# A two-layer trunk in split fp32: three conditioning vectors summed by transfers, residuals on VectorE, and tails of products in another order

## The chip, the cores and the metric

The kernel runs on one core of one Trainium2 chip. The metric is the device time of one execution in microseconds (us), the median of the runs shown. TensorE (PE) multiplies matrices; VectorE (DVE), ScalarE (ACT) and GpSimd (POOL) work on tiles; SyncE (SP) issues most of the transfers (DMA). Each engine carries out its own instructions in program order and waits for the others at semaphores.

## The reference

256 tokens of 1024 elements pass two layers. Each layer has a mixer and a "peer" block, each between a modulation and a residual with a layer norm. All is float32, batch 1.

```python
for i in range(2):
    sh1, sc1, g1, sh2, sc2, g2 = split(silu(c) @ ada_w[i] + ada_b[i], 6)   # conditioning vectors of 1024
    hx = xs * (1 + sc1) + sh1
    if i == 0:                       # mixer 0: hc is the modulated context
        q, k, v, gu, gv = split(hx @ w_in); k_c, v_c = split(hc @ w_in[:, 1024:3072])
        a = head_rms(softmax(q1 k1) v - lam * softmax(q2 k2) v)       # 8 heads, rope on q and k
        yx = concat(a, gelu(gu) * spatial(layer_norm(gelu(gv)))) @ w_out
    else:                            # mixer 1: window means as a fixed 256x256 matrix per group
        yx = (grouped(multiscale_pool(hx @ w_in), w_grp) * scale) @ w_out
    xs = layer_norm(alpha * xs + g1 * yx) * ln_g[i,0] + ln_b[i,0]
    hx = xs * (1 + sc2) + sh2
    # peer: 8 heads choose 16 of 16384 experts by two top-16 lists of keys
    f = sum over chosen (softmax(best) * gelu(hx @ u[idx])) * v[idx]
    xs = layer_norm(alpha * xs + g2 * f) * ln_g[i,1] + ln_b[i,1]
```

The peer blocks are computed densely: all 16384 rows of u and of v are read, and a gate that is zero outside the chosen experts stands between.

## The kernel before

Products keep float32 precision by splitting each operand into a rounded high part and a low part, hi and lo, and adding three products (hi·hi, lo·hi, hi·lo) in PSUM. The weights come as a list of items, each a tile of 128x1024 float32 (512 KB): 8 for the first two conditioning vectors twice, 32 for the first mixer's input, 12 for its output, then for each peer 16 query tiles (wq), 2 of keys, 128 of u and 128 of v, and between the peers 8 + 2 + 2 + 8 for the pool mixer. `run_items` goes through the list. For each item SP loads `raw` (four slots), ScalarE copies it to `hi`, VectorE or GpSimd (`lo="v"` or `"g"`) subtracts to `lo` (three slots of hi and lo), TensorE multiplies. Splits are issued as far ahead as the slots allow. `hold` and `release` keep them back at the ends of stages, and the last items of an output product use tiles of their own, `xhi` and `xlo`. There is no scheduler: the order on each engine is that in which the program issues.

The first mixer's attention goes in four groups of two heads, each with two k items, two q items and two v items; `rope` copies the rows in exchanged order with ScalarE (`rp`) and multiplies on VectorE (`rt`). Between the items of the groups stand the score units (`scores`, `turn`, `mix`), and the steps of three conditioning vectors of layer 0 (j = 2, 3, 4): `ada` loads eight row tiles `aw` of 128x1024, and VectorE sums them, each multiplied with the 128 values of silu(c) that belong to it, into `aacc`. At its `end` a product with ones adds the 128 partitions: as a row (j = 2, stored to DRAM as `grow`, the gate) or as a column (j = 3, 4). `chained` puts a vector's end behind the first step of the next. Seven more vectors are made in the same way during the first peer's v.

`rowsum_product` multiplies activations as the stationary operand with an item's rows into four accumulators (two token blocks nb by two column halves c). With `half` the last five items are kept so that the four accumulators finish one after another: (0,0), (0,1), (1,0), (1,1), and `norm_part` begins a block's residual and statistics behind each; `norm_end` makes the reciprocal root on VectorE in steps of 128x1 (L173 to L189) and normalises into `x`. `to_hT` transposes x on TensorE, scales the result, and splits it into the `h` tiles that the next product reads. Where a mixer ends (`mixed`), block 0 is transposed, block 1 is normalised, and `settle_block` then transposes block 1 and stores x for the peer's residual (`xhd`). I call these places seams: the first from mixer 0 to peer 0, the second from peer 0 to the pool mixer, the third from the pool mixer to peer 1.

The peer's residual adds alpha·ln_b to x·alpha·ln_g: `residual(i)` is called while v items 92, 98 and 104 are multiplied. The pool mixer's is made in `second_rest`. `mid` splits the pool mixer's first product z, which the fixed pool matrix then multiplies.

Of the kernel before, what the change touches and what calls it, by code (L numbers as in the profile page):

```python
# [34 lines left out]
class Build:  # L35
# [6 lines left out]


# [12 lines left out]
    def split(self, it):  # L56
# [6 lines left out]
        eng.tensor_sub(lo, it["raw"], hi.bitcast(FT))  # L63
# [147 lines left out]
    def norm_part(self, nb, c):  # L211
# [8 lines left out]
        (nc.vector if nb and c else nc.gpsimd).tensor_tensor(t[:, s], t[:, s], ln["res"][nb][:, s], op=OP.add)  # L220
# [34 lines left out]
    def to_hT(self, nb, sc, bi, full, late=False):  # L255
# [6 lines left out]
        for q in range(2):  # L262
# [18 lines left out]
            (nc.gpsimd if nb == 0 and (q or late) else nc.vector).tensor_sub(lo, x, hi.bitcast(FT))  # L281
# [12 lines left out]
    def rowsum_product(self, acc, w_rows, stat, lo="v", order=None, after=None, half=None, early=False, own=None, owned=0, hold=True):  # L294
# [11 lines left out]
        def product(i, k, hi, lo_t, nb, cols=HALVES):  # L306
            s = again[i, nb] if (i, nb) in again else stat(k, nb)
            again[i, nb] = s
            for part, (x, w) in enumerate(((0, hi), (1, hi), (0, lo_t))):
                for a, b in cols:  # L310
                    nc.tensor.matmul(acc[2 * nb + a // 512], s[x], w[:, a:b], start=i == 0 and part == 0, stop=i == last and part == 2)  # L311
        again = {}
        for i, k in enumerate(ks):
            def run(hi, lo_t, i=i, k=k):
# [42 lines left out]
    def ada(self, pool, l, j, kind, dst, ahead=1):  # L357
# [6 lines left out]
        def load(k):  # L364
            w = st["w", k] = pool.tile([128, 1024], FT, name="aw", bufs=3)
# [26 lines left out]
        def go(i):  # L392
            if i < 8:
                load(i)
            elif i == 8 and kind == "row":
                w = st["w", 8] = pool.tile([128, 1024], FT, name="aw", bufs=3)
# [6 lines left out]
    def chained(vectors):  # L403

        q, end = [], None
        for steps, e in vectors:
            for i, s in enumerate(steps):
                q.append([end, s] if i == 1 and end else [s])
            end = e
        q += [[], [], [end]]  # L410
# [50 lines left out]
    def first(self):  # L461
# [107 lines left out]
        def others():  # L569

            P = st["P"]
            st["ada"] = self.chained([self.ada(P, 0, j, *(("row", self.growd[0][0]) if j == 2 else ("col", self.adac[:, 0, j])))
                                      for j in (2, 3, 4)])

        def ada_step(n=1):
            for _ in range(n):
                f = st["ada"] and st["ada"].popleft()
                if f:
                    f()

# [73 lines left out]
        for t in range(4):  # L654
# [7 lines left out]
            def after(t=t):  # L662
# [8 lines left out]
                if t == 3:  # L671
                    pe.close()
                    others()
                    st["K"] = pt_.enter_context(tc.tile_pool(name="kq", bufs=1))
# [23 lines left out]
        def scores(g, h, nb):  # L698
# [15 lines left out]
            for m, p in enumerate(ps):  # L714
                nc.vector.tensor_reduce(mx[:, m, 0:1], p, axis=AX.X, op=OP.max, negate=True)
                x = T.tile([128, 512], FT, name="ex", bufs=6)
# [751 lines left out]
```

## Time and profile before

| | |
|---|---|
| median of 3 runs | 2044.43 us (2044.4 to 2045.88) |
| profiled execution | 2044.35 us, its span 2042.5 us |
| mean granted TensorE clock | 0.985 |
| TensorE busy | 1963.7 us |
| VectorE busy | 1559.4 us |
| ScalarE busy | 970.3 us |
| GpSimd busy | 377.9 us |
| DMA | 389.93 MB, 191 GB/s |

A row of the profile's timeline has the start, the time taken, the engine, the line of the kernel, the operation, the tiles written and read with their shapes, how many it groups, and in brackets how long the engine sat idle before it and what ended that. "<-DVE lo L63" is VectorE's instruction of line 63 that writes lo. A row of the waits has the engine and its instruction, what it waited for, the total, how often, and the longest. A row of `MATMUL` with x4 has the time from the first start to the last end.

### The profile page before, as it was taken

The numbers are of one execution on the slowest core, as the hardware profiler recorded it, in microseconds if no ns is written. First come the engines' busy times: TensorE is split into PE (matmuls) and PEld (weight loads), VectorE is DVE, ScalarE is ACT, GpSimd is POOL, SyncE is SP. The second block draws the span as 40 slices with busy tenths as digits, with TensorE's granted clock in tenths as the row PEclk, the third lists the DMA queues.
The fourth block names the chain that finished last, engine by engine and source line by source line (L and its number), as shares of the span: only waits on it lengthen the run. The fifth ranks groups of instructions, "written<-read, shape, count | busy, mean of one in ns | idle before, by whom it ended". The sixth has DMA issues, their size and how long they took to land.

```text
span 2042.5 us, 34071 instructions
## 1 busy us (share of the span) xinstructions
PE 1963.7 (96%) x13348; PEld 1773.0 (87%) x13348; DVE 1559.4 (76%) x2740; ACT 970.3 (48%) x1354; POOL 377.9 (19%) x171
## 2 busy tenths in 40 slices
PE   7799979999999999999999889999999999999997
PEld 4789869999999998888778779999999998888886
DVE  6878868999888757777777769998888755555566
ACT  6444544454544445444445454445544444444443
POOL 0100027792000000000011436891000000000031
PEclk9899989999999999999999889999999999999999
DMA  8534345555444558888876444555444556666663
GB/s 307 213 135 154 105 136 175 173 178 166 156 152 149 167 184 281 295 298 291 291 275 215 146 156 164 177 178 162 156 153 148 175 177 195 195 194 192 219 239 116
DMA packets 108178, 389.93 MB, mean 191 GB/s; under 512 B 12777, under 2 KB 12905, under 8 KB 108017
## 3 DMA queue, kind: packets, MB, share of 16 engines
q1 hardware_dynamic: 105992, 384.37, 56.6%
q10 hardware_dynamic: 2024, 3.38, 0.6%
q8 instruction: 104, 1.70, 0.4%
q14 instruction: 58, 0.47, 0.1%
HBM read 384.55 MB, written 3.16 MB: 190 GB/s over the span
## 4 chain that ended last, share of the span: by engine, by line
PE 64%; DVE 25%; issue 5%; DMA 2%; ACT 2%; POOL 1%; SPq 0%; DVEq 0%; ACTq 0%; POOLq 0%
PE pa L311 26%; PE px L311 8%; PE pa L957 8%; PE pa L958 8%; PE pa L961 8%; PE pt L1109 2%; DVE lo L63 2%; DVE oh L1036 1%; DVE oh L1041 1%; DVE topi L987 1%; DVE sc L988 1%; PE pa L598 1%; DVE topi L990 1%; PE pa L852 1%; ACT hi L61 1%
## 5 line engine op out<-in xcount | busy, mean ns | idle before, releaser
L61 ACT ACTIVATE hi<-raw 128x1024 fp32r<-128x1024 f32 x599 | 632.7, 1059 | 579.8 <-PE px L311 358.9
L63 DVE TENSOR_TENSOR lo<-raw,hi 128x1024 fp32r<-128x1024 f32 x487 | 614.6, 1264 | 362.6 <-ACT hi L61 361.6
L957 PE MATMUL pa<-h,hi 128*128 128x256 f32 x2304 | 578.4, 289 | 2.1 <-DVE h L280 2.1
L958 PE MATMUL pa<-h,hi 128*128 128x256 f32 x2304 | 566.7, 284 | 0.5 <-DVE h L281 0.5
L311 PE MATMUL pa<-hi,h 128*128 128x512 f32 x1524 | 471.7, 391 | 1.6 <-ACT h L278 1.6
L957 PEld LDWEIGHTS pa<-h,hi 128*128 128x128 f32 x2304 | 442.5, 192 | 2.9 <-DVE h L280 2.9
L958 PEld LDWEIGHTS pa<-h,hi 128*128 128x128 f32 x2304 | 443.2, 192 | 1.0 <-issue 1.0
L311 PEld LDWEIGHTS pa<-hi,h 128*128 128x128 f32 x1524 | 286.0, 188 | 64.5 <-ACT h L278 1.8
L961 PE MATMUL pa<-h,lo 128*128 128x256 f32 x2304 | 324.5, 284 | 0.0
L63 POOL TENSOR_TENSOR lo<-raw,hi 128x1024 fp32r<-128x1024 f32 x112 | 287.8, 2586 | 79.6 <-ACT hi L61 78.1
L961 PEld LDWEIGHTS pa<-h,lo 128*128 128x128 f32 x2304 | 298.8, 193 | 0.0
L311 PE MATMUL pa<-lo,h 128*128 128x512 f32 x762 | 255.7, 390 | 0.0
L1243 POOL TENSOR_SCALAR ln_g<-ln_g 128x1024 f32<-128x1024 f32 x2 | 5.6, 2778 | 1143.7 <-DMA ln_g<-in_ln_g 577.3
L311 PE MATMUL px<-hi,h 128*128 128x512 f32 x508 | 197.7, 389 | 0.0
L311 PEld LDWEIGHTS pa<-lo,h 128*128 128x128 f32 x762 | 143.3, 188 | 29.9
L1123 ACT ACTIVATE A<-pt 128x256 f32<-128x256 f32 (+31 forms) x182 | 50.9, 310 | 227.3 <-DVE A L1121 216.0
L311 PEld LDWEIGHTS px<-hi,h 128*128 128x128 f32 x508 | 95.3, 188 | 19.8
L1100 DVE TENSOR_TENSOR m<-e,gd 128x512 f16<-128x512 f16 x256 | 105.4, 454 | 2.2
L311 PE MATMUL px<-lo,h 128*128 128x512 f32 x254 | 98.8, 389 | 0.0
L375 DVE SCALAR_TENSOR_TENSOR aacc<-aw,csil,aacc 128x1024 f32<-128x1024 f32 x70 | 89.5, 1279 | 4.2 <-DMA aw<-in_ada_w 4.1
L1109 PE MATMUL pt<-m,e 128*128 128x128 f16 x1024 | 81.6, 220 | 3.1 <-DVE m L1100 0.9
L155 DVE TENSOR_TENSOR h<-A,h 128x1024 fp32r<-128x1024 f32 (+1 forms) x66 | 81.0, 1227 | 1.4 <-ACT h L154 1.4
(369 smaller groups left out, 2130.6 us busy)
## 6 DMA issues: line engine op xcount, KB each, us to landing
raw<-in_uT SPq DMA_DIRECT2D x256, 512.0 KB, 3.5
raw<-in_peer_v SPq DMA_DIRECT2D x256, 512.0 KB, 4.4
aw<-in_ada_w SPq DMA_DIRECT2D x80, 512.0 KB, 5.3
raw<-in_w_in SPq DMA_DIRECT2D x32, 512.0 KB, 5.5
raw<-in_wq SPq DMA_DIRECT2D x32, 512.0 KB, 3.6
raw<-in_ab_w_out SPq DMA_DIRECT2D x12, 512.0 KB, 3.6
raw<-in_ada_w SPq DMA_DIRECT2D x8, 512.0 KB, 5.9
xraw<-in_ada_w SPq DMA_DIRECT2D x8, 512.0 KB, 5.2
```

Source lines behind the costliest of these rows:

```text
L61: nc.scalar.activation(hi, it["raw"], AF.Copy)
L63: eng.tensor_sub(lo, it["raw"], hi.bitcast(FT))
L155: self.nc.vector.tensor_sub(lo, src, hi.bitcast(FT))
L311: nc.tensor.matmul(acc[2 * nb + a // 512], s[x], w[:, a:b], start=i == 0 and part == 0, stop=i == last and part == 2)
L375: nc.vector.scalar_tensor_tensor(st["acc"], w, c, st["acc"], op0=OP.mult, op1=OP.add)
L598: nc.tensor.matmul(o, (hi, lo)[x][:, 128 * k:128 * k + 128], f(k)[y], start=k == 0 and part == 0, stop=k == 7 and part == 2)
L957: mm(out, hi[:, cs], hh, start=k == 0, stop=False)
L958: mm(out, hi[:, cs], hl, start=False, stop=False)
L961: mm(out, lo[:, cs], self.h(k)[0], start=False, stop=k == 7)
L1100: nc.vector.tensor_tensor(v4(x), v4(st["e1"][:, s]), wide(st["gd"][i], ch, 4), op=OP.mult)
L1109: nc.tensor.matmul(p[:, 128 * j:128 * j + 128], e2[:, j], m[i][:, j], start=i == 0, stop=i == 1)
L1123: nc.scalar.activation(x[:, e:], y[:, e:], AF.Copy, scale=1.0 / 4096)
```

## The change

It consists of eleven edits.

1. The three vectors of the first mixer: ScalarE multiplies each tile `aw` with its column of silu(c) (the first into `aacc`, the others in place), and GpSimd issues a transfer that adds the tile to `aacc` in SBUF (`accum_op=add`), 21 in all. `aacc` has two buffers, `aw` four, the loads run two steps ahead, a vector's end stands behind the third step of the next.
2. `norm_part`: both sums of a residual on VectorE.
3. `to_hT`: its lo always on VectorE; for block 0 of `mixed` they are put off (`rest`) until behind `norm_end(1)`.
4. The lo of items that are split between `norm_end(0)` and `settle_block` are put off behind the transposes of block 1 (`lows`). The first three wq items' lo go to VectorE.
5. The store of x (`xhd`) goes from SP's queue to GpSimd's.
6. The first three items of pool_w_in: all of block 0's products, ordered by part, then the transposes of block 1, then its products.
7. The last item of pool_w_in finishes column half by column half, and `mid` follows that order.
8. The peer's residual: two VectorE operations per row instead of GpSimd's three.
9. The pool mixer's residual: four VectorE operations, one behind each of the first four items of pool_w_out, instead of six on GpSimd.
10. The first mixer's residual and gate are loaded at the first output item instead of the fourth, into tiles of the vectors.
11. The attention's exponentials have five buffers instead of six, the squares one instead of two.

```diff
@@ split
-        eng.tensor_sub(lo, it["raw"], hi.bitcast(FT))
+        low = functools.partial(eng.tensor_sub, lo, it["raw"], hi.bitcast(FT))
+        if self.lows is None:
+            low()
+        else:
+            self.lows.append(low)
@@ norm_part
-        (nc.vector if nb and c else nc.gpsimd).tensor_tensor(t[:, s], t[:, s], ln["res"][nb][:, s], op=OP.add)
+        nc.vector.tensor_add(t[:, s], t[:, s], ln["res"][nb][:, s])
@@ to_hT
-            (nc.gpsimd if nb == 0 and (q or late) else nc.vector).tensor_sub(lo, x, hi.bitcast(FT))
+            low = functools.partial(nc.vector.tensor_sub, lo, x, hi.bitcast(FT))
+            if rest is None:
+                low()
+            else:
+                rest.append(low)
@@ rowsum_product, run
-                    if i == EARLY - 1:
-                        self.settle_block()
-                    product(*x, 0)
                     tail.append(x)
                     if i == EARLY - 1:
-                        for x in tail:
-                            product(*x, 1)
+                        for part in (0, 2, 1):
+                            for x in tail:
+                                product(*x, 0, parts=(part,))
+                        self.settle_block()
+                        for part in (0, 2, 1):
+                            for x in tail:
+                                product(*x, 1, parts=(part,))
...
+                elif half is None and i == last:
+                    for c in HALVES:
+                        for nb in range(2):
+                            product(*x, nb, [c])
@@ ada, step
             if k == 0:
-                st["acc"] = pool.tile([128, 1024], FT, name="aacc", bufs=1)
+                st["acc"] = (dma or pool).tile([128, 1024], FT, name="aacc", bufs=2 if dma else 1)
+            if dma:
+
+                nc.scalar.activation(w if k else st["acc"], w, AF.Copy, scale=c)
+                if k:
+                    nc.gpsimd.dma_start(st["acc"], w, accum_op=OP.add)
+            elif k == 0:
                 nc.vector.tensor_scalar(st["acc"], w, c, None, op0=OP.mult)
@@ first, others
-            st["ada"] = self.chained([self.ada(P, 0, j, *(("row", self.growd[0][0]) if j == 2 else ("col", self.adac[:, 0, j])))
-                                      for j in (2, 3, 4)])
+            st["ada"] = self.chained([self.ada(P, 0, j, *(("row", self.growd[0][0]) if j == 2 else ("col", self.adac[:, 0, j])),
+                                               ahead=2, dma=st["K"]) for j in (2, 3, 4)], 2)
+            ada_step(2)
@@ first, after of the output items
-            if next(left) == 3:
-                assert st["unit"] == 20 and not self.next and not st["ada"]
-                st["cols"]()
-                pt_.close()
-                L = st["L"] = pl.enter_context(tc.tile_pool(name="late", bufs=1))
-                st["res"] = [L.tile([128, 1024], FT, name=f"res{i}") for i in range(2)]
-                st["grow"] = L.tile([128, 1024], FT, name="grow")
+            k = next(left)
+            if k == 8:
+
+                assert not st["ada"]
+                *st["res"], st["grow"] = [st["P"].tile([128, 1024], FT, name="aw", bufs=4) for _ in range(3)]
...
+                st["cols"]()
+            if k == 11:
                 for r in st["res"]:
                     nc.scalar.activation(r, r, AF.Copy, scale=ALPHA)
@@ mixed
+            self.lows = []
...
-        self.to_hT(0, hs, hb, st["full"], late=True)
+        rest = []
+        self.to_hT(0, hs, hb, st["full"], rest)
...
         def settle_block():
+            for f in rest:
+                f()
             self.to_hT(1, hs, hb, st["full"])
+            for f in self.lows:
+                f()
+            self.lows = None
             for i in range(2):
-                nc.sync.dma_start(self.xhd[l][i], self.ln["x"][i])
+                nc.gpsimd.dma_start(self.xhd[l][i], self.ln["x"][i])
@@ peer, wq items
-            self.item(a["wq"][l, j], run, after=after, budget=2.4, lo="g")
+            self.item(a["wq"][l, j], run, after=after, budget=2.4, lo="v" if j < 3 else "g")
@@ peer, residual
-            nc.gpsimd.tensor_scalar(row, row, ALPHA, None, op0=OP.mult)
             for nb in range(2):
-                nc.gpsimd.tensor_tensor(st["xa"][nb], st["xa"][nb], row, op=op)
+                y, z = (row, st["xa"][nb]) if op == OP.add else (st["xa"][nb], row)
+                nc.vector.scalar_tensor_tensor(st["xa"][nb], y, ALPHA, z, op0=OP.mult, op1=op)
@@ second_rest
-            nc.gpsimd.tensor_scalar(r, r, ALPHA, None, op0=OP.mult)
...
-            nc.gpsimd.tensor_tensor(st["res"][i], ts[i], rows[0], op=OP.mult)
-            nc.gpsimd.tensor_tensor(st["res"][i], st["res"][i], rows[1], op=OP.add)
+        def residual(j):
+
+            i, r = j // 2, st["res"][j // 2]
+            x, y, op = (rows[1], r, OP.add) if j % 2 else (ts[i], rows[0], OP.mult)
+            nc.vector.scalar_tensor_tensor(r, x, ALPHA, y, op0=OP.mult, op1=op)
...
+        st["residual"] = deque(functools.partial(residual, j) for j in range(4))
@@ second, mid
-                nb, c = divmod(b, 2)
+                c, nb = divmod(b, 2)
...
-        self.rowsum_product(acc, rows, stat, half=half, own=lambda: st.get("L"), owned=TAIL)
+
+        def after():
+            if st["residual"]:
+                st["residual"].popleft()()
+        self.rowsum_product(acc, rows, stat, half=half, after=after, own=lambda: st.get("L"), owned=TAIL)
```

How it moves instructions is shown at three places. On ScalarE, group 0 of the first mixer before, from the copies that rope needs (L684, `rp`) to the next group of them; `kT` is the context's keys, `sl` the exponentials of the lambda:

```order
L684 ACTIVATE rp<-pa 32x512 x4
L154 ACTIVATE kT_797<-pa 128x2x256
L508 ACT_TABLE_LOAD
L508 ACTIVATE sl<-sl 128x2
L61 ACTIVATE hi<-raw 128x1024 x2
L684 ACTIVATE rp<-pa 32x512 x4
```

And now, from the item's hi ahead of it:

```order
L393 ACTIVATE aacc<-aw,csil 128x1024
L393 ACTIVATE aw<-aw,csil 128x1024
L64 ACTIVATE hi<-raw 128x1024
L393 ACTIVATE aw<-aw,csil 128x1024 x2
L709 ACTIVATE rp<-pa 32x512 x4
L161 ACTIVATE kT_805<-pa 128x2x256
L532 ACT_TABLE_LOAD
L532 ACTIVATE sl<-sl 128x2
L64 ACTIVATE hi<-raw 128x1024
L393 ACTIVATE aw<-aw,csil 128x1024
L64 ACTIVATE hi<-raw 128x1024
L393 ACTIVATE aw<-aw,csil 128x1024
```

Four scalings stand ahead of the first rope and two ahead of the next. On TensorE, the second seam before, with the transposes of block 0 (`aw`) and block 1 (`aacc`) and the products of the first three items of pool_w_in:

```order
L266 MATMUL pt<-ident,aw 128x128 x8
L311 MATMUL pa<-hi,h 128x512 x4
L311 MATMUL pa<-lo,h 128x512 x2
L311 MATMUL pa<-hi,h 128x512 x4
L311 MATMUL pa<-lo,h 128x512 x2
L266 MATMUL pt<-ident,aacc 128x128 x8
L311 MATMUL pa<-hi,h 128x512 x4
L311 MATMUL pa<-lo,h 128x512 x2
```

And now:

```order
L273 MATMUL pt<-ident,aw 128x128 x8
L323 MATMUL pa<-hi,h 128x512 x6
L323 MATMUL pa<-lo,h 128x512 x6
L323 MATMUL pa<-hi,h 128x512 x6
L273 MATMUL pt<-ident,aacc 128x128 x8
```

The transposes of block 1 moved behind the third item's products. On VectorE, the pool mixer's output product up to the first multiplication with the gate (`rt`), before:

```order
L63 TENSOR_TENSOR lo<-raw,hi 128x1024
L155 TENSOR_TENSOR y_12250<-yf,y_12249 128x512 x2
L63 TENSOR_TENSOR lo<-raw,hi 128x1024
L63 TENSOR_TENSOR xlo<-raw,xhi 128x1024 x5
L219 TENSOR_TENSOR rt_12639<-pa,grow 128x512 x2
L225 BN_STATS n_st<-rt_12639 128x6 x2
```

And now, where `xs` is the residual:

```order
L68 TENSOR_TENSOR xlo<-raw,xhi 128x1024
L1344 SCALAR_TENSOR_TENSOR xs_12254<-aw,ln_g 128x1024
L68 TENSOR_TENSOR xlo<-raw,xhi 128x1024 x2
L1344 SCALAR_TENSOR_TENSOR xs_12254<-ln_b,xs_12254 128x1024
L68 TENSOR_TENSOR xlo<-raw,xhi 128x1024 x2
L1344 SCALAR_TENSOR_TENSOR xs_12255<-aacc,ln_g 128x1024
L1344 SCALAR_TENSOR_TENSOR xs_12255<-ln_b,xs_12255 128x1024
L226 TENSOR_TENSOR rt_12656<-pa,grow 128x512
L227 TENSOR_TENSOR rt_12656<-rt_12656,xs_12254 128x512
```

The four residual operations stand between the xlo, the last two right ahead of the gate.

More of the change, by code (lines that the diff above doesn't have):

```diff
@@ L253, in norm_end, with to_hT @@
             yield s
-    def to_hT(self, nb, sc, bi, full, late=False):
+    def to_hT(self, nb, sc, bi, full, rest=None):
         nc = self.nc
@@ L304, in rowsum_product, with product @@
         tail = []
-        def product(i, k, hi, lo_t, nb, cols=HALVES):
+        def product(i, k, hi, lo_t, nb, cols=HALVES, parts=range(3)):
             s = again[i, nb] if (i, nb) in again else stat(k, nb)
             again[i, nb] = s
-            for part, (x, w) in enumerate(((0, hi), (1, hi), (0, lo_t))):
+            for part in parts:
+                x, w = ((0, hi), (1, hi), (0, lo_t))[part]
                 for a, b in cols:
@@ L354, in rowsum_product, with ada @@
             self.holds += 1
-    def ada(self, pool, l, j, kind, dst, ahead=1):
+    def ada(self, pool, l, j, kind, dst, ahead=1, dma=False):
         nc = self.nc
@@ L364, in load @@
         def load(k):
-            w = st["w", k] = pool.tile([128, 1024], FT, name="aw", bufs=3)
+            w = st["w", k] = pool.tile([128, 1024], FT, name="aw", bufs=4 if dma else 3)
             nc.sync.dma_start(w, self.a["ada_w"][l, 128 * k:128 * k + 128, 1024 * j:1024 * j + 1024])
@@ L395, in go @@
             elif i == 8 and kind == "row":
-                w = st["w", 8] = pool.tile([128, 1024], FT, name="aw", bufs=3)
+                w = st["w", 8] = pool.tile([128, 1024], FT, name="aw", bufs=4 if dma else 3)
                 nc.sync.dma_start(w[0:1], self.a["ada_b"][l:l + 1, 1024 * j:1024 * j + 1024])
@@ L402, in chained @@
     @staticmethod
-    def chained(vectors):
+    def chained(vectors, at=1):
         q, end = [], None
@@ L407, in chained @@
             for i, s in enumerate(steps):
-                q.append([end, s] if i == 1 and end else [s])
+                q.append([end, s] if i == at and end else [s])
             end = e
-        q += [[], [], [end]]
+        q += [[]] * (at + 1) + [[end]]
         return deque(lambda fs=fs: [f() for f in fs] for fs in q)
@@ L715, in scores @@
                 nc.vector.tensor_reduce(mx[:, m, 0:1], p, axis=AX.X, op=OP.max, negate=True)
[L716 removed]
+                x = T.tile([128, 512], FT, name=f"ex{m}", bufs=3 - m)
                 nc.scalar.activation(x, p, AF.Exp, bias=mx[:, m, 0:1], accum_out=sums[m])
@@ L740, in mix @@
             if h == 0:
-                st["sq"] = T.tile([128, 2, 256], FT, name="sq", bufs=2)
+                st["sq"] = T.tile([128, 2, 256], FT, name="sq", bufs=1)
                 st["og"] = T.tile([128, 2, 256], FT, name="og", bufs=2)
@@ L893, in after @@
                 nc.sync.dma_start(st["grow"], self.growd[0][0].to_broadcast([128, 1024]))
-            elif st.get("L") and st["unit"] == 20:
-                st["unit"] = 21
+                st["cols"]()
+            if k == 11:
                 for r in st["res"]:
                     nc.scalar.activation(r, r, AF.Copy, scale=ALPHA)
+            if k == 3:
+                assert st["unit"] == 20 and not self.next
+                pt_.close()
+                st["L"] = pl.enter_context(tc.tile_pool(name="late", bufs=1))
         self.rowsum_product(acc, rows, stat, order=order, after=after, half=half,
```

14 lines of the change are left out of this document (8 added, 6 removed).

## The prediction

> **What bounds the kernel now.** I read the page first, then the busy time by stretches, the waits of the stretches where TensorE falls back, and their timeline. TensorE runs 96% of the span, so only what shortens its idle time, or the half-clock stretch after it, can shorten the kernel.
>
> ```profile
> span 2042.5 us, 34071 instructions
> PE 1963.7 (96%) x13348; PEld 1773.0 (87%) x13348; DVE 1559.4 (76%) x2740; ACT 970.3 (48%) x1354; POOL 377.9 (19%) x171
> L61 ACT ACTIVATE hi<-raw 128x1024 fp32r<-128x1024 f32 x599 | 632.7, 1059 | 579.8 <-PE px L311 358.9
> L63 DVE TENSOR_TENSOR lo<-raw,hi 128x1024 fp32r<-128x1024 f32 x487 | 614.6, 1264 | 362.6 <-ACT hi L61 361.6
> ```
>
> 2042.5 − 1963.7 = 79 us of idle time is all there is, and much of it is the start and the end. The profiled execution took 2044.35 us, 0.08 below the median of 2044.43, so a sum against it needs no shift. A difference under 0.2% (4 us) I count as no change.
>
> Three kinds of stretches lose time: the first mixer around 60 to 236 us, the seams where a mixer's tail is normalised, and the middle of the pool mixer.
>
> ```profile
> 62.00:236.00 174.00, 157.46 (x1214) 146.15 (x1215) 143.72 (x234) 77.23 (x142) 0.28 (x1) 0.96 0.43 149
> 80.00:90.00 10.00, 5.01 (x36) 4.51 (x34) 9.69 (x17) 0.15 (x1) 0.00 (x0) 0.92 0.17 58
> 90.00:100.00 10.00, 6.70 (x36) 6.70 (x37) 9.83 (x13) 3.85 (x6) 0.00 (x0) 0.57 0.83 289
> 290.00:300.00 10.00, 3.81 (x16) 3.01 (x16) 8.24 (x19) 6.88 (x15) 4.83 (x3) 0.50 0.28 106
> 1200.00:1210.00 10.00, 3.12 (x17) 2.15 (x16) 8.61 (x20) 7.32 (x14) 4.82 (x3) 0.73 0.13 52
> ```
>
> The columns are the stretch, its length, busy time of PE, weight loads, DVE, ACT and POOL, granted clock, DMA share and GB/s. In the mixer TensorE is idle 174 − 157.5 = 16.5 us, VectorE busy 143.7, ScalarE only 77.2, GpSimd not at all. After each long idle the granted clock falls to about a half.
>
> **Conditioning vectors off VectorE.**
>
> ```profile
> L375 DVE SCALAR_TENSOR_TENSOR aacc<-aw,csil,aacc x21: 1276/1280/1285, 74.1 to 209.0; 128x1024 f32<-128x1024 f32 x21
> PE pa L852 <- DVE lo L63: 8.3, 2, 4.7
> DVE aacc L375 <- DMA aw<-in_ada_w: 4.1, 1, 4.1
> 70.60 2.39 ACT L684 ACTIVATE rp<-pa 32x512 f32<-32x512 f32 x4 [2.77 <-PE pa L598]
> 74.10 1.28 ACT L508 ACT_TABLE_LOAD   x1
> 79.50 1.28 DVE L375 SCALAR_TENSOR_TENSOR aacc<-aw,csil,aacc 128x1024 f32<-128x1024 f32 x1 [4.13 <-DMA aw<-in_ada_w]
> 82.16 0.68 DVE L650 TENSOR_TENSOR sgt<-pt,sgu_b 128x512 f32<-128x512 f32 x1
> 87.18 1.22 DVE L63 TENSOR_TENSOR lo<-raw,hi 128x1024 fp32r<-128x1024 f32 x1
> 93.31 1.22 PE L852 MATMUL pa<-lo,h 128*128 128x256 f32 x4 [3.63 <-DVE lo L63]
> ```
>
> VectorE loses 21 × 1.28 = 26.9 us and three first scalings. ScalarE gains 24 scalings; its 1.06 us copy of the same size is the row for one, so 25 us, and 77.2 + 25 of 174 is still far from full. What pays is only what stood in front of a late lo. In group 0 (8.3 us of waits in two) VectorE loses 1.28, the 4.13 us wait and 1.28 again between 74.1 and 80.7, 6.7 us. But ScalarE now runs four scalings ahead of the rope copies, and the last two wait for loads that land some 5.3 us after their issue: rope starts near 74.4 instead of 70.60, with 2.4 for it, 0.6 for kT and 1.5 for the table and exponential 78.9. VectorE's gating takes 5.0 us (82.16 to 87.18), behind it the lo: done at 85.6 instead of 88.4, and the second wait ends at 89.3 instead of 93.3. That is −4.0, with −0.5 for the clock of the next stretch.
>
> ```profile
> PE pa L852 <- DVE lo L63: 3.2, 1, 3.2
> 163.72 1.84 PE L382 MATMUL pt<-ones,aacc 128*128 128x1 f32 x16
> 168.24 2.18 PE L598 MATMUL pa<-h,hi 128*128 128x256 f32 x16
> aw<-in_ada_w SPq DMA_DIRECT2D x80, 512.0 KB, 5.3
> xhd<-xh SPq DMA_DIRECT2D x4, 512.0 KB, 2.6
> ```
>
> In group 1 (3.2 us) two scalings, 2.1 us, stand ahead of the rope, which VectorE's rt waits for; against two 1.28 us sums saved that is 0. Groups 2 and 3 give −1.5 together with their rest. The accumulating transfers have no row. The nearest is a load of the same 512 KB, 5.3 us, which writes SBUF but does not read it; the upper bound is set below in the rivals, the lower is 2.6 us, that of a store, which reads SBUF and writes none. I take 5.3, since the transfer has to write a 128x1024 tile as the load does and its source is nearer, while the tile that it adds to must be read too. The sum of a vector ends with the last two, one behind the other on GpSimd's queue: scaled by about 159.5, landed at 159.5 + 2 × 5.3 = 170.1, while the ones products (moved behind the first q item) are due at about 163.7 + 5.8 = 169.5: +0.6. −4.0 − 0.5 − 1.5 + 0.6 is −5.4; VectorE's end of the row vector, moved one step back as well, I count at −0.6, so **−6**. The bounds are −12 (the 16.5 us of idle time less what TensorE's own sequence and the first rope leave) and +1 (ScalarE takes back all but the accumulation's wait).
>
> With the vectors go their buffers: the sum's tile is doubled, the loads get a fourth slot and run two steps ahead instead of one, and to make room the exponentials' ring shrinks from six tiles to five and the squares' from two to one. A score unit makes two exponentials and the older one is read by its transposes two units later, so three and two tiles hold what is live; the squares are read within the same unit's group. I cost both at 0, covered by the four items between two groups. On SP's queue the loads of a step stand where they stood, one step earlier; on GpSimd's queue there is no other work in this stage (0.28 us busy), so the 21 transfers delay nobody but each other.
>
> In sentences of their own: the Trainium skill, "DMA: Bandwidth & Descriptors", section "Anatomy of one DMA — SWDGE (gpsimd) path", fits a GpSimd-issued transfer by 2.0 us + bytes / 436 GB/s, an estimate of 3.2 us here, by which the +0.6 would vanish. No run here shows one yet.
>
> **First seam (mixer 0 to peer 0).**
>
> ```profile
> 281.47 1.29 DVE L219 TENSOR_TENSOR rt<-pa,grow 128x512 f32<-128x512 f32 x2 [3.90 <-DMA grow<-grow]
> 282.31 2.55 POOL L220 TENSOR_TENSOR rt<-rt,res 128x512 f32<-128x512 f32 x2 [220.03 <-DVE rt L219]
> 292.29 1.62 DVE L176 SCALAR_TENSOR_TENSOR rs_r<-rs_y,n_ve 128x1 f32<-128x1 f32 x1
> 297.44 1.97 PE L266 MATMUL pt<-ident,xh 128*128 128x128 f32 x8 [5.60 <-DVE xh L249]
> 300.48 0.58 PE L957 MATMUL pa<-h,hi 128*128 128x256 f32 x1 [1.07 <-DVE h L280]
> ```
>
> The gate row now comes eight items earlier: its 3.9 us wait goes, and the first multiplication starts at about 278, when its product is done. The two residual sums move from GpSimd (1.3 each) to VectorE (0.69 by its own row of that line). The products of rows 128 to 255 end where they did (near 286.6), so the second half's norm cannot start earlier; what shrinks there is the reciprocal root, whose tiny steps take up to 1.62 us beside GpSimd's work and 0.2 without it, about 3 us over all of them. The GpSimd work (three lo of items, two of the transposed block) moves behind the second block's transposes. The three residual and gate loads go into the vectors' slots at the first output item instead of the fourth; SP issues them some 35 us earlier, ahead of the output weights, of which four are loaded ahead, so that costs nothing while TensorE spends 2.7 us on an item and a load takes 5.3 with several under way. ScalarE's two scalings of the residual (1.06 each) move from the last items into the middle, where it idles half the time (48% of the span busy). The store of the normalised rows goes from SP's queue to GpSimd's: SP, which held the next weights behind a store that waits for the second block, is free for the first query weights, and GpSimd's lo of the fourth query item waits behind the store instead, some 0.4 us of issue, hidden by three VectorE lo ahead of it. What eats part of the gain is VectorE: the deferred lo of the first block and of three items, 2 × 0.69 and 3 × 1.26 us, now stand around the second block's own. With ScalarE's chain for the first block now the limit, the product starts at about 295.7 instead of 300.48: **−4.8**, bounds −3 (the gate wait alone, less the deferred lo) and −6 (gate wait and root).
>
> **Second seam (peer 0 to pool mixer).**
>
> ```profile
> 1140.61 1.03 PE L266 MATMUL pt<-ident,aacc 128*128 128x128 f32 x8
> 1143.13 0.50 PE L311 MATMUL pa<-hi,h 128*128 128x512 f32 x1
> ```
>
> The transposes of the second block now stand behind all 18 products of the first, 18 × 0.23 us from about 1136, some at the half clock, so near 1142.0 instead of 1140.6; its own products then start at 1144.5: **+1.4**, bounds 0 (the faster root on VectorE) and +2.
>
> **Pool mixer, the z split.**
>
> ```profile
> 1153.90 9.94 DVE L63 TENSOR_TENSOR lo<-raw,hi 128x1024 fp32r<-128x1024 f32 x3 [0.86 <-ACT hi L61]
> 1156.17 3.26 POOL L1308 TENSOR_TENSOR xs<-xs,ln_b 128x1024 f32<-128x1024 f32 x1
> 1164.50 0.58 PE L151 MATMUL pt<-hi,xlo 128*128 128x256 f32 x1 [2.89 <-DVE xlo L155]
> 1170.13 0.41 PE L150 MATMUL pt<-lo,xhi 128*128 128x256 f32 x1
> ```
>
> Three lo take 3.3 us each instead of 1.26 while GpSimd makes the residual, and z's xlo comes 2.9 us late; TensorE then issues a 256-wide product every 0.21 us up to 1170, against 0.12 later, some 27 products, so 2.6 us. GpSimd's six operations become four on VectorE in the next product: the stall goes, and with the last item finished column half by column half the split starts sooner. −2.9 − 2.6 + 0.5 for the split's own chain: **−5.0**, bounds −3 and −6.
>
> **Third seam.**
>
> ```profile
> 1191.03 1.23 DVE L63 TENSOR_TENSOR xlo<-raw,xhi 128x1024 fp32r<-128x1024 f32 x1 [0.53 <-ACT xhi L61]
> 1209.22 1.97 PE L266 MATMUL pt<-ident,xh 128*128 128x128 f32 x8 [6.21 <-DVE xh L249]
> ```
>
> The same shortening as at the first seam, about 3 us of slowed root steps, would start the query product earlier. But of the four residual sums, one popped behind each of the first four items, the last two stand on VectorE right behind the last xlo (done at 1192.3) and ahead of the first multiplication: 2 × 1.28 = 2.56 us, and two sums that GpSimd did beside it, 2 × 0.69, come on top. 2.56 + 1.38 − 3.0 leaves about +0.9, of which the earlier lo of the next weights gives back 0.2. **+0.7**, bounds −2 and +1.
>
> **Peer residual on VectorE.**
>
> ```profile
> 1065.66 0.42 SPq L1242 DMA_DIRECT2D ln_b<-in_ln_b  x1
> 1069.46 1.23 DVE L63 TENSOR_TENSOR lo<-raw,hi 128x1024 fp32r<-128x1024 f32 x1 [1.50 <-ACT hi L61]
> 1071.89 2.77 POOL L1243 TENSOR_SCALAR ln_b<-ln_b 128x1024 f32<-128x1024 f32 x1 [11.21 <-DMA ln_b<-in_ln_b]
> 1074.97 0.62 PE L311 MATMUL pa<-lo,h 128*128 128x512 f32 x2
> ```
>
> The wait for the row moves onto VectorE. From its issue at 1065.66 to 1071.89 nothing behind it runs; two sums bring that to 1074.4, and the lo that ran at 1069.46 is done at about 1075.7, wanted at 1074.97: +0.75 per layer, after which 1.23 of 2.72 us per item catches up. Two layers **+1.5**, bounds 0 (three lo tiles hide it) and +4. ln_g's wait is the same, six items earlier in the same order; it is in these figures. At the end of the kernel the first block's two sums stand on VectorE in front of the last root: +0.3. In the routing the first three query items' lo on VectorE, 1.26 us against 2.6 on GpSimd, let the queries start sooner: −0.5. Together **−0.2**.
>
> **Sum.** −6 − 4.8 + 1.4 − 5.0 + 0.7 + 1.5 − 0.2 = −12.4, so 2044.35 − 12.4 = **2032.0 us**.
>
> **Rivals.** ScalarE gives the relief back: its scalings wait for loads, and every hi behind them with them. For it speaks that each group's rope sits behind two to four of them; against it, the 97 us in which it idles (174 − 77.2). It decides where rope starts later than 77.4: 74.4 puts the gating at 79.2, 3.0 ahead of the 82.16 of now. The mixer then gives 0: 2032 + 6 = 2038.
>
> The accumulating transfer is longer than a load. At 8 us each the ones products wait: 159.5 + 16 = 175.5 against 169.5, 6 us, and similarly in part for the other two ends. With the mixer's gain of 6 spent and about 6 more, 2044: no change.
>
> Slower: all 21 go one behind the other, from about 69 us to the last product of v at about 235, so 166 / 21 = 7.9 us each is what the stage holds. Each us above costs 21 us; at 9 us 189 − 166 = 23, thus about 2055. It decides from 8.7 us, where 0.8 × 21 = 17 outweighs 12.4 and the 4 of no change. Against this rival stand 5.3 us and a DMA share of 0.43; for it, that the transfer must also read what it adds to.
>
> The Trainium skill, "SBUF — State Buffer", section "SBUF: two separate sides", speaks for this rival: a GpSimd-issued transfer's descriptors wait while VectorE runs a copy or tensor_scalar in its two-port mode. No row here shows such a transfer; VectorE's 143.7 of 174 us hold few copies.
>
> All stalls go and the clock stays up: the mixer gives 12, the third seam 2, the peers nothing: 2032 − 6 − 2.7 − 1.5 ≈ 2022.
>
> **How the numbers follow.** The weights are how many rows speak for each: three of the seven terms rest on rows that stand beside the work itself, the accumulation on none. My forecast 55% (own range 2026 to 2039), the better case 10%, ScalarE's 17%, no change 11%, slower 7%. Faster is 55 + 10 + 17 = 82%. The range leaves out the slow tail and half of the no-change case: 2019 to 2042.
>
> **What would show it.** Right: the residual rows on VectorE with 1.28 us, z's wait gone, the seam's product near 296, lo waits of the mixer under 8 us. Wrong: TensorE waiting at the ones products, ScalarE's scalings waiting for GpSimd's transfers, VectorE idle for ln_b over 6 us with TensorE idle behind it.

## Result: slower by 1.1%, because the sums by transfer run late

| | before | after |
|---|---|---|
| median | 2044.41 us (4 runs, 2043.35 to 2045.88) | 2066.82 us (4 runs, 2065.47 to 2067.13) |
| ratio | | 1.0107, 95% interval 1.0095 to 1.0118 |
| profiled execution, span | 2044.35, 2042.5 us | 2067.13, 2065.4 us |

The page of the changed kernel, then its waits of TensorE and one each of SP and GpSimd from 60 to 266 us, in which the first mixer's input product lies, then busy times (columns as in the prediction) of that stretch and of one stop in it:

```profile
span 2065.4 us, 34116 instructions
PE 1972.1 (95%) x13348; PEld 1777.8 (86%) x13348; DVE 1532.7 (74%) x2751; ACT 995.3 (48%) x1378; POOL 309.2 (15%) x155
PE pt L406 <- DMA aacc<-aw: 13.3, 1, 13.3
PE pt L413 <- DMA aacc<-aw: 11.6, 1, 11.6
PE pa L877 <- DVE lo L68: 6.8, 3, 2.9
PE pa L877 <- ACT hi L64: 5.4, 3, 3.5
SPq L384 <- DMA aacc<-aw: 77.0, 13, 8.8
POOL aacc L395 <- DMA aacc<-aw: 77.2, 11, 8.8
60.00:266.00 206.00, 167.92 (x1238) 155.85 (x1236) 121.91 (x214) 107.58 (x173) 22.97 (x25) 0.88 0.68 179
116.80:128.40 11.60, 0.03 (x1) 0.03 (x2) 0.00 (x0) 0.00 (x0) 0.86 (x1) 0.68 0.76 176
```

The same stretch before, up to the first output product, and TensorE's longest wait in it:

```profile
60.00:235.20 175.20, 157.81 (x1221) 146.44 (x1219) 144.99 (x234) 78.19 (x144) 2.29 (x1) 0.96 0.43 148
PE pa L852 <- DVE lo L63: 13.6, 5, 4.7
```

VectorE was relieved as said (lo waits 6.8 us where they were 13.6), but TensorE stands still twice for the products with ones (L413 the row, L406 a column), because the accumulating transfers of their vector have not landed. In the stop shown no engine but GpSimd does anything. ScalarE waits too, so that hi comes late afterwards, and SP waits 77 us for slots that hold tiles not yet added, so that the vectors' next loads are issued late. No copy to hi waits for its own load in this stretch. TensorE is idle for 38.1 us of this stretch (206 − 167.9), against 17.4 us of 175.2 before, and the granted clock is 0.88 instead of 0.96, while its own work grew from 157.8 to 167.9 us. These are the 30.8 us by which the stretch is longer: 20.7 of idle time (24.9 by the two stops, less what the relief gave) and 10.1 of longer work. The transfers, and the first stop in the timeline:

```profile
aacc<-aw POOLq DMA_DIRECT2D x21, 512.0 KB, 8.0
DMA to landing us min/median/max: 4.5/8.0/10.2
76.45 2.39 ACT L709 ACTIVATE rp<-pa 32x512 f32<-32x512 f32 x4
114.07 0.86 POOL L395 DMA_DIRECT2D aacc<-aw  x1 [6.74 <-DMA aacc<-aw]
120.29 0.86 POOL L395 DMA_DIRECT2D aacc<-aw  x1 [5.36 <-DMA aacc<-aw]
128.37 3.22 PE L413 MATMUL pt<-aacc,ones 128*1 128x512 f32 x4 [11.58 <-DMA aacc<-aw]
132.88 1.15 ACT L393 ACTIVATE aacc<-aw,csil 128x1024 f32<-128x1024 f32 x1 [20.63 <-DVE aw L414]
194.06 3.55 PE L406 MATMUL pt<-ones,aacc 128*128 128x1 f32 x16 [13.35 <-DMA aacc<-aw]
```

Within a vector no transfer is issued before the one ahead of it has landed, and 11 of them waited for just that (77.2 us): 6.2 us from one to the next here, 8.1 to the products, and from the first issue at 70.1 to the last at 248.3 it is 8.9 us on average, the waits for ScalarE among them. The store of the row stands on ScalarE's queue behind VectorE's addition, which is why ScalarE sat 20.63 us; before, it sat 7.8 us at that place. The products themselves then take 3.22 and 3.55 us at the lowered clock, against 1.88 and 1.84 before.

Most of the rest of the change did what was forecast. Rows of the changed kernel that answer to those of before: the first seam, the second, z, the third, and the peer's residual:

```profile
307.59 0.69 DVE L226 TENSOR_TENSOR rt<-pa,aw 128x512 f32<-128x512 f32 x1 [0.59 <-PE pa L323]
314.01 0.22 DVE L183 SCALAR_TENSOR_TENSOR rs_r<-rs_y,n_ve 128x1 f32<-128x1 f32 x1
321.19 1.11 PE L273 MATMUL pt<-ident,xh 128*128 128x128 f32 x4 [3.24 <-DVE xh L256]
324.82 0.58 PE L991 MATMUL pa<-h,hi 128*128 128x256 f32 x1 [0.64 <-DVE h L287]
1167.78 1.03 PE L273 MATMUL pt<-ident,aacc 128*128 128x128 f32 x8
1188.29 1.88 DVE L162 TENSOR_TENSOR xlo<-pa,xhi 128x512 fp32r<-128x512 f32 x3
1189.26 0.28 PE L158 MATMUL pt<-hi,xlo 128*128 128x256 f32 x1
1215.67 1.23 DVE L1344 SCALAR_TENSOR_TENSOR xs<-ln_b,xs 128x1024 f32<-128x1024 f32 x1
1229.79 1.11 PE L273 MATMUL pt<-ident,xh 128*128 128x128 f32 x4 [3.24 <-DVE xh L256]
1096.63 2.36 DVE L1279 SCALAR_TENSOR_TENSOR xa<-ln_b,xa 128x1024 f32<-128x1024 f32 x2 [2.95 <-DMA ln_b<-in_ln_b]
```

The gate is waited for no longer, the root's steps take 0.22 us, the transposes of the third seam wait 3.24 instead of 6.21 us, z's xlo comes without a wait and the products behind it 0.12 us apart. The starts of the same TensorE instructions in both timelines give the account by stage:

| stage, up to | before | after | change | forecast |
|---|---|---|---|---|
| first output product of mixer 0 | 235.18 | 265.98 | +30.8 | −6 |
| first query product of peer 0 | 300.48 | 324.82 | −6.5 | −4.8 |
| second seam's transposes of block 0 | 1133.26 | 1159.07 | +1.5 | +0.5 |
| block 1's first pool product into px | 1143.47 | 1170.64 | +1.4 | +1.4 |
| first product of z | 1161.22 | 1189.02 | +0.6 | (next line) |
| first px product of pool_w_out | 1180.42 | 1202.28 | −5.9 | −5.0 |
| first query product of peer 1 | 1212.25 | 1233.41 | −0.7 | +0.7 |
| last product | 2029.40 | 2051.85 | +1.3 | +0.5 |
| end of the span | 2042.5 | 2065.4 | +0.4 | +0.3 |

All but the first line make −7.9. The first line decided.

### The profile page after: what moved, and what is told of

Its sections match the earlier page's. It is cut to its first block, busy times and chain, and to the rows that moved or that the text cites. A ratio compares the mean times of both kernels' runs of the same rounds, so it can differ in the third digit from the quotient of the medians.

```text
span 2065.4 us, 34116 instructions
## 1 busy us (share of the span) xinstructions
PE 1972.1 (95%) x13348; PEld 1777.8 (86%) x13348; DVE 1532.7 (74%) x2751; ACT 995.3 (48%) x1378; POOL 309.2 (15%) x155
## 4 chain that ended last, share of the span: by engine, by line
PE 64%; DVE 23%; DMA 6%; ACT 4%; issue 3%; POOL 0%; SPq 0%; ACTq 0%; DVEq 0%; POOLq 0%
PE pa L323 26%; PE px L323 8%; PE pa L991 7%; PE pa L995 7%; PE pa L992 7%; DMA aacc<-aw 4%; PE pt L1143 2%; DVE lo L68 2%; ACT hi L64 2%; PE pa L877 1%; DVE oh L1070 1%; DVE oh L1075 1%; DVE topi L1021 1%; DVE sc L1022 1%; DVE topi L1024 1%
## 5 line engine op out<-in xcount | busy, mean ns | idle before, releaser
L68 DVE TENSOR_TENSOR lo<-raw,hi 128x1024 fp32r<-128x1024 f32 x491 | 599.5, 1224 | 377.2 <-ACT hi L64 375.2
L68 POOL TENSOR_TENSOR lo<-raw,hi 128x1024 fp32r<-128x1024 f32 x106 | 272.0, 2583 | 81.0 <-ACT hi L64 80.8
L259 POOL TENSOR_TENSOR aw<-aw 128x512 f32<-128x512 f32 x4 | 5.3, 1344 | 644.1 <-ACT aw L254 644.0
```

What stands on the lines that cost most here:

```text
L68: low()
```

## Experiments

Medians of the kernel before beside these runs were 2043.5 to 2044.7 us.

**The vectors on VectorE again, and the transfers alone.** The first takes the sums by transfer out of the change, the second puts them alone into the kernel before.

```diff
 # first: the changed kernel with
-  ... ahead=2, dma=st["K"]) for j in (2, 3, 4)], 2)
-            ada_step(2)
+  ...) for j in (2, 3, 4)])
 # second: the kernel before with the edits 1 and 11
```

> The changed kernel, but the three vectors of the first mixer are summed on VectorE again, as before the change; the other ten edits stay (the smaller rings of exponentials and squares too). Theory one, the chain: the first mixer's 30.8 us of loss come from the 21 transfers one behind the other, so all of it goes and the rest of the change keeps what its stages show, 24.3 - 30.8 + the later stages = about -8 against before: 2036 us. Rival: the loss comes from what was moved along with them (smaller rings, loads two steps earlier, the first mixer's residual loads); then at most part of it goes and the time stays over 2044 us.

> The kernel before, with the sums of the three vectors by scaling and accumulating transfers alone (and the smaller rings that make the room); nothing else of the change. Theory one, the chain: 2044.4 + 31 = 2075 us, since no other edit touches that stage. Rival, that the transfers only hurt together with the other edits: 2044 to 2055 us.

Measured: 2037.84 us (ratio 0.9965, 0.9951 to 0.9979) and 2072.58 us (1.0137, 1.0121 to 1.0154). In the second, TensorE's longest waits from 60 to 265 us are the same two stops:

```profile
PE pt L388 <- DMA aacc<-aw: 13.0, 1, 13.0
PE pt L395 <- DMA aacc<-aw: 10.0, 1, 10.0
```

So the ten other edits are worth −6.8 us (against 2044.66 beside them) and the sums by transfer cost 28 to 29, with or without them. The smaller rings and the moved residual loads stay in the first kernel, so they are out as causes. The vectors' loads two steps ahead, the later products with ones and ScalarE's scalings went and came together with the transfers, so these two runs do not part them; the runs at the lower pace below keep the scalings and the loads two steps ahead and are faster than before.

**What a transfer costs by itself.** Seven stages, each six transfers, with nothing else of the kernel.

> No computation of the reference: seven stages one after the other, each six GpSimd-issued transfers within SBUF, one behind the other on the same tile: A 512 KB accumulating, alone; B 512 KB plain; C as A beside VectorE's subtractions of two SBUF tiles; D as A beside VectorE's copies of float32 tiles; E as A beside 20 loads of 512 KB from HBM; F as A in two chains; G 256 KB accumulating. Theory one, latency of the transfer itself: A about 7 us each, C and D the same, E 8 to 9, F two in the time of one, G more than half of A, B less than A. Rival, descriptors that wait for VectorE: A about 3 to 4, C or D 8 and more. Rival, the traffic of the loads: A 3 to 4, E 8.

The median to landing in each stage, the first load of the kernel, and two issues of stage A and D:

```profile
accA<-srcA POOLq DMA_DIRECT2D x6, 512.0 KB, 4.5
accB<-srcB POOLq DMA_DIRECT2D x6, 512.0 KB, 2.9
accC<-srcC POOLq DMA_DIRECT2D x6, 512.0 KB, 4.5
accD<-srcD POOLq DMA_DIRECT2D x6, 512.0 KB, 4.8
accE<-srcE POOLq DMA_DIRECT2D x6, 512.0 KB, 8.1
accF<-srcF POOLq DMA_DIRECT2D x6, 512.0 KB, 5.4
accG<-srcG POOLq DMA_DIRECT2D x6, 256.0 KB, 3.3
base<-in_x SPq DMA_DIRECT2D x1, 512.0 KB, 3.2
12.68 0.86 POOL L56 DMA_DIRECT2D accA<-srcA  x1 [3.92 <-DMA accA<-srcA]
116.65 1.16 POOL L56 DMA_DIRECT2D accD<-srcD  x1 [3.97 <-DMA accD<-srcD]
```

An accumulating transfer alone takes 4.5 us, where a plain one takes 2.9 and a load from HBM 3.2. VectorE's subtractions do nothing to it, its copies 0.3 us, all of it in the issue (0.86 to 1.16). Beside a stream of loads it takes 8.1, about the 8.0 of the kernel, which speaks for the third theory, the traffic of the loads; that the two figures are so close is in part chance, since by the trace's packets about 2.4 MB of loads start between issue and landing of each of the first four transfers of stage E, and about 1.05 MB in the seven of the kernel's that took 7.1 to 9.1 us. The two of the kernel's 21 with under 0.1 MB of loads beside them took 4.5 us. Theory one was wrong in its size alone (4.5, not 7) and right on the other stages; the 7 us of latency that it needed is not there. The Trainium skill, "DMA: Bandwidth & Descriptors", section "Anatomy of one DMA — SWDGE (gpsimd) path", gives 3.2 us for 512 KB by its fit, an estimate: the plain transfer comes near it (2.9), the accumulating one does not (4.5). The Trainium skill, "SBUF — State Buffer", section "SBUF: two separate sides", has descriptors wait while VectorE copies in the two-port mode: the trace agrees in direction, but the size is 0.3 us of 4.8, far too little for the 8 us.

**Two chains.** Each vector has two sums, for even and odd tiles.

```diff
+                y = st["accs"][k % 2]
+                nc.scalar.activation(w if k > 1 else y, w, AF.Copy, scale=c)
+                if k > 1:
+                    nc.gpsimd.dma_start(y, w, accum_op=OP.add)
```

> The changed kernel, but each vector has two sums, for even and for odd tiles, so that a transfer waits for the one before the last; 18 transfers instead of 21, and TensorE's products with ones are doubled (+1.8 us for each vector at most). Theory one in the form that the 8 us are latency: two are under way at a time, about 4.3 us for each, 18 of them take 77 us of 165, both waits for the ends go: 2031 to 2042 us. Rival, that 8 us is what the transfer keeps the engines busy (data or descriptors): two at a time take as long as two in a row, 144 us and late again at the ends: 2055 us or more.

Measured: 2043.75 us, no different from before (1.0001, 0.9991 to 1.0011). Waits of TensorE and SP from 60 to 241 us, the transfers, and one of the products:

```profile
PE pa L881 <- DVE lo L68: 6.4, 3, 2.4
PE pa L881 <- ACT hi L64: 4.5, 3, 3.5
SPq L384 <- DMA aacc<-aw: 21.5, 7, 7.9
aacc<-aw POOLq DMA_DIRECT2D x18, 512.0 KB, 7.6
166.89 3.64 PE L409 MATMUL pt<-ones,aacc 128*128 128x1 f32 x32
```

Both stops are gone, though a transfer still takes 7.6 us; so the wait of one transfer for the one before it was what made the sums late (there are also three fewer of them; what that gives by itself is not shown). The mixer still ends 5.0 us later than before (240.21 against 235.18). TensorE's idle time fell from 17.4 to 11.8 us, with 6.4 us of waits for lo and 4.5 for hi where 13.6 for lo stood. But its own work grew from 157.8 to 168.4 us: some 5.5 by the doubled products with ones (3.6 us three times instead of 1.85), and the granted clock is 0.93 instead of 0.96. The time came out 1.75 us above the expectation.

**Pace and place.** The first kernel takes one step per item instead of two at the k items, sets the products with ones four steps later and the residual's loads five items later; of the other two each does one of the first two, the place alone and the pace alone, and all three have the later residual loads, which no run tries by themselves.

```diff
-                    ada_step(2)
+                    ada_step()                 # pace; not in the second kernel
-  ... for j in (2, 3, 4)], 2)
+  ... for j in (2, 3, 4)], 6)                  # place; not in the third kernel
-            if k == 8:                         # residual loads, all three kernels
+            if k == 1:
```

> The changed kernel with the same 21 transfers in one chain, but spread: one step per item instead of two at the k items, the products with ones four steps later (the third vector's behind the tenth output item), the residual loads five items later. Theory one, that the transfers hurt only where TensorE's products with ones and ScalarE's queue stand behind a late sum: the two stops of 11.6 and 13.3 us and the half clock behind them go, the mixer loses at most 3 us against before, the seam gives up 1 to 3: 2034 to 2043 us. Rival, the transfers' traffic delays the weights and with them every hi: the mixer stays 15 us or more behind, over 2050 us.

> As the kernel of the late ends, but two steps at each k item again, as in the changed kernel: only the products with ones stand later (behind the seventh step of the next vector, the third vector's behind the second output item). Theory one, that the distance between a vector's last transfer and its products decides: both stops go, 2022 to 2030 us. Rival, that the pace decides, with 32 steps in the four groups asking for more than a chain of 8 us each can give: the chain falls behind and the third vector's products or the weights wait, 2035 to 2055 us.

> As the kernel of the late ends, but the products with ones stand behind the third step of the next vector again, as in the changed kernel; only the pace is lower, one step per item. Theory one, the pace: the transfers have fewer loads beside them (5.9 us instead of 8.0) and are done before the products, 2022 to 2030 us. Rival, the distance: two stops of 5 us and more stay, 2035 us or more.

Measured: 2023.22 us (0.9905, 0.989 to 0.992), 2044.98 us (1.001, 1.0 to 1.002) and 2029.29 us (0.9923, 0.9902 to 0.9944). Of the first: busy times of the mixer's stretch, the transfers, SP's wait there; of the second, whose profile fell on one of the longest of its ten runs (2050.25 us): TensorE's and SP's longest waits, two of ScalarE, and the transfers; of the third: TensorE's and SP's, and the transfers:

```profile
60.00:217.30 157.30, 150.41 (x1190) 140.54 (x1188) 118.69 (x207) 98.13 (x163) 16.42 (x17) 0.99 0.76 211
aacc<-aw POOLq DMA_DIRECT2D x21, 512.0 KB, 5.9
SPq L384 <- DMA aacc<-aw: 31.1, 7, 8.6
```

```profile
PE pa L878 <- ACT hi L64: 14.1, 5, 8.5
SPq L384 <- DMA aacc<-aw: 85.2, 14, 9.1
ACT aw L393 <- DMA aw<-in_ada_w: 15.6, 5, 6.1
ACT aacc L393 <- DMA aw<-in_ada_w: 10.8, 2, 6.2
aacc<-aw POOLq DMA_DIRECT2D x21, 512.0 KB, 8.2
```

```profile
PE pt L406 <- DMA aacc<-aw: 4.7, 1, 4.7
SPq L384 <- DMA aacc<-aw: 13.9, 6, 4.9
aacc<-aw POOLq DMA_DIRECT2D x21, 512.0 KB, 6.0
```

The first came out far below its range (2034 to 2043). The same 21 transfers in one chain land in 5.9 us, TensorE never waits for them (SP still does, 31.1 us), and the stage before the output product ends at 217.30 instead of 235.18: 17.9 us earlier, more than any bound that I had. Of these, 1.84 us are the third vector's products with ones, which now stand in the output product. At the first query product it is 20.1 us (280.37 against 300.48), where the kernel with the sums on VectorE gains 6.2: the transfers, asked for slowly and used late, are worth about 14 us over VectorE's sums (14.6 between the medians). TensorE's idle time is 6.9 us and its granted clock 0.99, against 17.4 and 0.96 before.

Pace and place both count. At the later place the lower pace gives 21.8 us (2044.98 to 2023.22), at the lower pace the later place gives 6.1 (2029.29 to 2023.22), of which 4.7 is the last wait. The later place at the high pace, with the later residual loads, takes the change from 2066.82 to 2044.98, but then the wait moves: SP stands 85 us behind slots of the vectors, so the vectors' loads come late, ScalarE waits 26.4 us for them with its scalings, and the hi behind them on its queue are late (14.1 us, 8.5 of it at one item). So the second run fits its rival, with the wait at ScalarE's queue in place of the weights' loads.

Why a transfer takes 5.9 at the lower pace and 8.0 at the higher is not settled. It is not the mean traffic, for the stretch moves more at the lower pace, 211 GB/s against 179; which loads fall beside a transfer differs, and no run sets that alone.

**One vector by transfers.** On the kernel of the small terms (below).

> The kernel of small terms, but the third vector alone is summed by seven accumulating transfers, one in three items, and its products with ones stand behind the fourth output item; the first two vectors stay on VectorE, one step per item. Theory one, that a transfer costs nothing where nothing waits for it: VectorE is freed of 9 us of the mixer, the lo waits shrink, 0 to -4 us against the kernel of small terms: 2028 to 2033 us. Rival, that ScalarE's scalings and the traffic cost what VectorE gains whatever the spacing: 2034 to 2040 us.

Measured: 2036.2 us (0.9966, 0.9954 to 0.9978), against 2037.84, which the spread of the runs does not clearly part (2035.59 to 2037.87 and 2036.33 to 2039.06). The mixer gained 1.7 us up to the output product (230.71 against 232.40), and from there to the first query product 1.9 were given back: 1.84 are the third vector's products with ones, moved from the one stage to the other. So the forecast gain did not come, and the time lies in the rival's range; TensorE's waits for lo went only from 11.8 to 10.5 us.

**The small terms, and the best version.** The first edits sit on the kernel with the vectors on VectorE, the other two kernels on that of the late ends.

```diff
-                        for part in (0, 2, 1):
-                            for x in tail: product(*x, 0, parts=(part,))
-                        self.settle_block()
+                        for part in (0, 2, 1):
+                            if part == 1: self.settle_block()
+                            for x in tail: product(*x, 0, parts=(part,))
-                    residual((i - 92) // 6)       # row and operations
+                    residual((i - 92) // 6)       # row; operations at 101 and 107
+            self.item(a["pool_w_grp"][t], run, after=lambda: st["residual"].popleft()())
```

> The kernel of the first experiment (vectors on VectorE) with four of the change's edits placed otherwise: the transposes of block 1 behind 12 instead of 18 products of block 0 in the second seam; one query item's lo on VectorE instead of three; the peer's residual operations three v items behind the issue of their row; the pool mixer's residual begun two items earlier. If each small term is what its stage showed: -1.8 in the second seam, -0.8 in each routing, 0 to -1.6 in each v phase, -1 ahead of the third seam, together -4 to -7 against the first experiment: 2031 to 2034 us. Rival, that these places are not what sets those stages: 2037 to 2038 us.

> The kernel of the late ends with three of the four small moves: transposes of block 1 behind 12 products in the second seam, the peer's residual operations three items behind their row, the pool mixer's residual two items earlier; the query items' lo stay as in the change. If the small terms are what the stages showed, -0.4 to -2.5 against the late ends: 2020 to 2023 us.

> As the kernel before, but six query items' lo on VectorE instead of three. The routing of both peers grew by 1.25 us each with three on VectorE, and by 1.2 to 1.5 more with one: if GpSimd's lo beside VectorE's routing is what delays the queries, six give back 1 to 3 us, 2018 to 2022 us; if VectorE's own load is, +1 to +4, 2022 to 2027 us.

Measured: 2037.84 us (0.9971, 0.9961 to 0.9981), the same as without the small terms; 2022.02 (0.989, 0.9873 to 0.9907) and 2022.19 us (0.9891, 0.9873 to 0.9908). The first missed: the second seam took 11.2 instead of 12.9 us and both v phases lost their extra, 0.9 and 1.6 us, but each routing grew by another 1.4 us with one lo on VectorE. The second came as expected, but 1.2 us under the late ends is not clear of the runs' spread. The third lies where its two forecasts meet: of the three numbers tried, three and six are the same within the runs. With three or six the routing stays 0.9 to 2.1 us a layer above before; what sets it is open. 2022.0 us is the lowest median here, 21 us under before and 45 under the change, with the same accumulating transfers that made the change slower.

## Why the prediction was wrong

- The time lay outside the range, on the side of the rival called slower, which had 7%. Its mechanism is the one that came: 21 transfers one behind the other that the stage cannot hold. The first of the signs named for "wrong" came too, TensorE waiting at the ones products.
- The first step that failed is the price of the accumulating transfer. "I take 5.3", the median of the loads from HBM, measured 8.0. A load alone takes 3.2 and in the kernel 5.3, 1.66 times as much; the same factor on the 4.5 of an accumulating transfer alone would give an estimate of 7.5. The 4.5 was in no row of before, but that the load's 5.3 already held the traffic was: "its source is nearer" was no reason once the loads are what stretches it.
- The second is the path: "the 21 transfers delay nobody but each other". The price alone does not explain the time, since the rival with 8 us a transfer came out at 2044. It put two transfers in series at each vector's end and about 12 us of waits on TensorE. The runs showed a chain that is behind along the whole vector (11 of 21 transfers waited for the one before), two stops of 24.9 us together, ScalarE held 20.6 us behind the row's store, SP held 77 us at the vectors' slots, and a granted clock of 0.88, which with the longer work is 10.1 us.
- The bounds of that term, −12 to +1, were too low on their upper side: the change gave +30.8. They took in a late sum at one vector (+0.6) and left the price of 8 us to the rivals.
- The account "166 / 21 = 7.9" asked the right question, whether the stage holds the chain, but it is a mean over the stage. By it 8.0 us would have cost 2 us, and the point "from 8.7 us" came of it. What decided is the pace in the groups, two steps at each k item, and what stands behind the chain.
- The rival on ScalarE came in part. In group 0 its four scalings put rope at 76.45 (the first row of the timeline above), 2 us later than forecast and near the 77.4 at which it was to decide. The second lo wait there ended at 91.25 instead of 93.31, 2.1 us earlier where −4.0 was booked; the lo itself was forecast only 2.8 us earlier (85.6 against 88.4), so part of the 4.0 had no source. In the run with the place alone, scalings that wait for loads, and hi behind them, are what TensorE waits for.
- The better case, "all stalls go and the clock stays up", had 2022. The same transfers at the lower pace came to 2023.2, but by another sum (17.9 us in the mixer, not 12, while the peers still lose 0.9 and 1.8): that the numbers agree is luck.
- The seams and z were near in size and right in sign but for the third seam. There the residual operations ahead of the gate put the root 1.7 us later (3.9 were forecast), and from the root to the query product it took 2.4 less, so that −0.7 came instead of +0.7. The first seam gave 4.8 us in the experiment without transfers, the very number, and 6.5 in the change, beyond its bound of 6.
- Routing: −0.5 was forecast, about +1.2 a layer came. The peer's residual: VectorE waits 2.5 to 4.2 us for the row, and the v phase lost nothing by it in the change, 0.9 and 1.6 us in one profile of the first experiment.

## What to carry to other kernels

Price a transfer by what the same queue's transfers cost in that stage against alone, and ask first whether a serial chain of them keeps the pace at which the program asks for them, item by item and not on average. A chain that is too slow is paid at every queue that stands behind its tiles. Moving the consumer back took 21.8 us off the change but moved the wait to the next loads and the engine that works on them. Asking half as often at the busiest items, with the residual loads later, turned +22 us into −14, and with the consumer moved back as well into −20. Taking work off an engine that makes TensorE wait can pay twice, by the wait and by the clock: with 38.1, 17.4 and 6.9 us of idle time in this stage the granted clock was 0.88, 0.96 and 0.99. With two chains it was 0.93 at 11.8 us, so the idle time is not all that sets it.

## Not expected of the hardware

In the stages of the probe, an accumulating transfer within SBUF takes 4.5 us for 512 KB where a plain one takes 2.9, and 8.1 beside loads. VectorE's copies beside it lengthen its issue from 0.86 to 1.16 us, by which it lands at 4.8, and nothing else; VectorE's subtractions do not touch it (4.5).
